# Queries of two pairs of heads in one product of 384 columns, and a new written order for layer 1's input and attention

## The chip, the cores and the metric

One core of one Trainium2 chip runs the whole program in one launch. The metric is the device time of one execution in microseconds (us), the median of the runs. The core has four engines that matter here: TensorE (PE in the profile; the load of its weights is PEld), VectorE (DVE), ScalarE (ACT) and GpSimd (POOL); SyncE (SP) issues most transfers.

## The reference

Two layers of a transformer block on 512 tokens of width 1024, conditioned by a vector, beside 256 tokens of context. Cut to the parts of layer 1 that the change touches:

```python
# layer 0: Fourier and Hyena mixer and feed-forward network, for x (512 tokens) and ctx (256)
# layer 1: attention for x over x and ctx, then the feed-forward network for x
a_x = hx @ w_in                                   # 256 for queries, 128 + 32 for keys and values
q = (_rms_norm(a_x[..., :256], q_a_norm) @ w_uq).reshape(B, L, 16, 96)
q = _rms_norm(q, q_norm)                          # over the 96 of each head
q = concat([q[..., :64], _rope_2d(q[..., 64:], rope)])
kv = (_rms_norm(a_kv[..., :128], kv_a_norm) @ w_ukv).reshape(B, L, 16, 64 + 64)
k = _rms_norm(concat([kv[..., :64], k_pe for all heads]), k_norm)   # with rope where it is x
s = einsum('bqhd,bkhd->bhqk', q, k) * 96 ** -0.5  # 16 heads, 512 queries, 768 keys
o = einsum('bhqk,bkhv->bqhv', softmax(s), v)
x = x + g1 * (o @ w_o)
```

All is fp32.

## The kernel before

**Products.** A fp32 number is split in two fp32r parts, hi (on ACT, L296) and lo (on DVE, L301), and a product is three products of the parts (`mm3`, L321, L322, L323). So each weight is loaded to `wr`, converted to `wh` and subtracted to `wl` before TensorE can use it.

**Stages.** Layer 0 and its feed-forward network come first (to about 820 us), then layer 1's input (low-rank products of queries and keys/values, norms, tables of rotation), then attention (905 to 1114), then the feed-forward network. The order of every engine's instructions is the order in which the program calls its steps: tables of step names are written out as strings, and the tile scheduler is told to keep that order (`manual_schedule`). `IN2_ORDER` holds the steps from the end of layer 0's down-projection to the start of attention, with the down-projection's own products (DP), the low-rank products (QA, KV, PE) and the loads among them; `ORDER` holds attention. There are four such blocks in the program before; in the block of `ORDER` SP is not among the engines that keep the written order, so the scheduler places its loads.

**Attention.** The 16 heads go as 8 pairs, numbered 0 to 7 behind the step's name (`QT.3`). For a pair:

- LW, WA, WD load and split the weights w_uq, for two pairs at a time (L309, L296, L301).
- QT multiplies the query's low-rank tiles `qah`, `qal` (two halves of 256 rows) by the weights, for four tiles of 128 tokens, 192 columns each: 4 x 2 x 3 = 24 products into the PSUM tile `k2` (one buffer, 1024 columns, also used by UK). In the trace they are `k<-wh,qah` and its like.
- SQ squares the result (ACT), RD sums it (DVE, L1926), TB (L1918) and TX (L1922) multiply it with the tables `tabm` and `tabx` into the tile `t2`. TB, TX and SQ free `k2`.
- UK makes the pair's keys into `k2`; KSQ, KS, KH, KL square, sum and split them. NA, NB, RT make the norms' factors, U scales the queries, TR transposes them (TensorE), QC and QL split them.
- SC makes the scores of 128 keys by 512 queries (6 steps for each of two heads), EV scales and moves them to SBUF (ACT), MA, MB, MD, AR find the maxima, SU subtracts, EX is the exponential (ACT).
- VP and VE make the values. PW (L2062) multiplies values and exponentials, ON (L2073) sums the exponentials: both are column-tiled, four products of 32 rows of output side by side (128*32 in the profile), six steps each for a pair. A step shows as 8 records.
- ZC copies the sums, ZA brings them through DRAM into 128 x 8, RC is the reciprocal, ZB and ZD bring it back spread over the rows (tile R), DV multiplies (tile O), OH and OL split the result.
- LX, XA, XD load and split the output weights w_o; WO multiplies.

RP.1 (L1867) and RP.0 (L1864) are thin products that place the rotated part of the keys, `kp`, and its sums.

```python
def QT(c, p):
    c.q = K2()
    wh, wl = wq[p // 2]
    for t_ in range(4):
        for k in range(2):
            s, w = slice(128 * t_, 128 * t_ + 128), slice(384 * (p % 2) + 192 * k, ...)
            self.mm3(c.q[:, 256 * t_ : 256 * t_ + 192], qah[k][:, s], qal[k][:, s], wh[:, w], wl[:, w], k == 0, k == 1)
```

Of the kernel before, what the change touches and what calls it, by code (L numbers as in the profile page):

```python
# [21 lines left out]
P = 128  # L22
D = 1024
KD = 8
# [27 lines left out]
SU11.2 ZD.1 SC11.3 EV10.3 KS.4 EV11.3 MA0.3 KH0.4 SC12.3 KH1.4 KL0.4 SC13.3 EX10.2 SC14.3 NA.4 MB0.3 QT.5 EX11.2 DV.1 MD0.3 NB.4 EV12.3 WD.6 ON0.2
AR0.3 ON1.2 EV13.3 RT.4 ON2.2 LX2.7 EV14.3 ON3.2 MA1.3 ON4.2 U1.4 ON5.2 PW0.2 U0.4 SQ.5 SU00.3 PW1.2 ZC.2 TR1.4 OH.1 ZA.2 TR0.4 XA1.7 RD.5 SC15.3 TB.5
QC0.4 PW2.2 QC1.4 QL0.4 PW3.2 EV15.3 TX.5 EX00.3 PW4.2 MB1.3 PW5.2 OL.1 SC00.4 MD1.3 SC01.4 EV00.4 RC.2 SC02.4 AR1.3 SU01.3 EV01.4 ZB.2 SC03.4 EV02.4
UK.5 EV03.4 XD1.7 ZD.2 EX01.3 SC04.4 MA0.4 SC10.4 LX0.7 EV04.4 SC05.4 SU10.3 KSQ.5 SC11.4 EV10.4 KS.5 EV05.4 SU11.3 EX10.3 SC12.4 SC13.4 DV.2 EV11.4
NA.5 PW0.3 EX11.3 MB0.4 ON0.3 ON1.3 NB.5 ON2.3 MD0.4 EV12.4 PW1.3 RT.5 AR0.4 EV13.4 SC14.4 U0.5 KH0.5 MA1.4 TR0.5 U1.5 ON3.3 PW2.3 KL0.5 QC0.5 ON4.3
SU00.4 EV14.4 PW3.3 KH1.5 ON5.3 PW4.3 OH.2 QL0.5 ZC.3 PW5.3 KL1.5 EX00.4 ZA.3 SC15.4 OL.2 SC00.5 SU01.4 EV15.4 TR1.5 EV00.5 SC01.5 QC1.5 MB1.4 QT.6
EV01.5 EX01.4 QL1.5 RC.3 MD1.4 ZB.3 SC02.5 TB.6 SQ.6 AR1.4 SC03.5 EV02.5 RD.6 ZD.3 SC10.5 EV03.5 SC04.5 TX.6 EV10.5 MA0.5 UK.6 EV04.5 SU10.4 SC11.5
KSQ.6 SC05.5 EV11.5 KS.6 SU11.4 EV05.5 EX10.4 SC12.5 NA.6 SC13.5 DV.3 EX11.4 SC14.5 MB0.5 SC15.5 EV12.5 ON0.4 PW0.4 MD0.5 NB.6 EV13.5 RT.6 AR0.5 PW1.4
KH0.6 MA1.5 ON1.4 U1.6 PW2.4 U0.6 ON2.4 KL0.6 KH1.6 ON3.4 PW3.4 EV14.5 SU00.5 PW4.4 EV15.5 OH.3 ON4.4 MB1.5 ON5.4 EX00.5 TR0.6 TR1.6 SU01.5 QT.7 QC0.6  # L60
QC1.6 ZC.4 QL0.6 EX01.5 ZA.4 MD1.5 PW5.4 TB.7 AR1.5 SQ.7 SC00.6 OL.3 XA0.7 SC01.6 TX.7 EV00.6 SC02.6 RD.7 EV01.6 SC03.6 RC.4 EV02.6 SU10.5 ZB.4 SC04.6
EV03.6 SC10.6 EV04.6 SC05.6 SU11.5 ZD.4 EX10.5 UK.7 EV10.6 SC11.6 MA0.6 KSQ.7 SC12.6 XD0.7 EV05.6 KS.7 EX11.5 MB0.6 ON0.5 ON1.5 EV11.6 NA.7 ON2.5 DV.4
EV12.6 SC13.6 MD0.6 NB.7 KH0.7 ON3.5 RT.7 AR0.6 ON4.5 EV13.6 U0.7 SC14.6 U1.7 KL0.7 TR0.7 ON5.5 MA1.6 EV14.6 PW0.5 QC0.7 SU00.6 PW1.5 KH1.7 PW2.5 ZC.5
# [179 lines left out]
class Builder:  # L243
# [2478 lines left out]
```

## Time and profile before

| | us |
|---|---|
| median of 3 runs (1493.09 to 1493.64) | 1493.27 |
| the profiled execution | 1492.97 |
| its span | 1491.2 |
| TensorE busy | 1468.9 (99%) |
| DVE busy | 1257.8 (84%) |
| ACT busy | 727.4 (49%) |
| POOL busy | 230.0 (15%) |
| mean granted clock of TensorE | 0.994 |

The span runs from the first to the last instruction that the profiler saw; 1.8 us of the execution lie outside it. A row of TensorE's timeline gives start, length and shape; matmuls overlap in the records, so the time that one takes is read from the start of one to the start of the next. Where a row ends with [..], the engine was idle that long ahead of it, and what it names ended the idle time.

### The profile page before, as it was taken

The page shows a single profiled execution, that of the slowest core. Times are in us where ns is not written, and L with a number is a line of the kernel's source. Part 1 is how long each engine was busy: PE and PEld are TensorE (multiplying, and loading weights), DVE is VectorE, ACT ScalarE, POOL GpSimd, SP SyncE. Part 2 cuts the span into 40 slices and gives each one's busy share as a digit, 9 for nine tenths or more (in the row PEclk, how much of TensorE's full clock was granted, in tenths as well). Part 3 has the DMA queues.
Part 4 walks back from the last instruction along what each step waited for, and adds up shares of the span by engine and source line. Part 5 has one row for each costly group of instructions (what it writes and reads, how often), then busy time and mean ns, then how long its engine had stood idle before and what let it go on. Part 6 is the DMA issues. An engine that isn't in the chain of part 4 may idle for free.

```text
span 1491.2 us, 24094 instructions
## 1 busy us (share of the span) xinstructions
PE 1468.9 (99%) x9216; PEld 1279.2 (86%) x9216; DVE 1257.8 (84%) x2118; ACT 727.4 (49%) x1117; POOL 230.0 (15%) x396
## 2 busy tenths in 40 slices
PE   7999999999999999999999999999999999999998
PEld 4778889798999999999999888665659999989997
DVE  6899999999988988778878777899957997878885
ACT  3452234355443344334344347988936554444442
POOL 0101043011112121121220000111111221212100
PEclk8999999999999999999999999999999999999999
DMA  8425543764477787778887440010035566555543
GB/s 334 147 92 179 201 151 106 236 210 121 106 195 181 195 206 183 176 211 215 212 212 248 138 139 26 23 32 20 16 110 167 137 168 154 148 158 149 142 108 119
DMA packets 89903, 226.36 MB, mean 152 GB/s; under 512 B 12955, under 2 KB 20605, under 8 KB 88765
## 3 DMA queue, kind: packets, MB, share of 16 engines
q1 hardware_dynamic: 64573, 161.28, 32.3%
q0 software_dynamic: 25216, 63.55, 19.7%
q8 instruction: 72, 1.18, 0.3%
q14 instruction: 42, 0.34, 0.1%
HBM read 203.15 MB, written 21.64 MB: 151 GB/s over the span
## 4 chain that ended last, share of the span: by engine, by line
PE 87%; DVE 7%; DMA 2%; ACT 2%; issue 1%; SPq 0%; POOL 0%; DVEq 0%; ACTq 0%; POOLq 0%
PE mm L321 21%; PE mm L323 21%; PE mm L322 21%; PE ms L323 3%; PE ms L321 3%; PE ms L322 3%; PE pv L2062 3%; PE s L2010 1%; PE pv L2073 1%; DVE wl L301 1%; PE s L321 1%; DMA sb<-wmodT 1%; PE s L322 1%; DVE junk L420 1%; PE s L323 1%
## 5 line engine op out<-in xcount | busy, mean ns | idle before, releaser
L296 ACT ACTIVATE wh<-wr 128x1024 fp32r<-128x1024 f32 (+4 forms) x179 | 153.2, 861 | 195.2 <-PE mm L322 89.8
L321 PE MATMUL mm<-hh,wh 128*128 128x512 f32 (+3 forms) x704 | 230.8, 328 | 0.7 <-ACT pt L1750 0.7
L322 PE MATMUL mm<-hl,wh 128*128 128x512 f32 (+3 forms) x704 | 228.6, 325 | 0.0
L323 PE MATMUL mm<-hh,wl 128*128 128x512 f32 (+3 forms) x704 | 227.9, 324 | 0.1
L301 DVE TENSOR_TENSOR wl<-wr,wh 128x1024 fp32r<-128x1024 f32 (+4 forms) x179 | 174.8, 981 | 47.6 <-ACT wh L296 47.2
L321 PEld LDWEIGHTS mm<-hh,wh 128*128 128x128 f32 x704 | 133.2, 189 | 12.2 <-issue 2.7
L322 PEld LDWEIGHTS mm<-hl,wh 128*128 128x128 f32 x704 | 133.2, 189 | 8.5 <-issue 0.4
L323 PEld LDWEIGHTS mm<-hh,wl 128*128 128x128 f32 x704 | 132.9, 189 | 8.7 <-DVE wl L301 0.8
L420 DVE SCALAR_TENSOR_TENSOR junk<-wr,sb 128x1024 bf16<-128x1024 f32 x96 | 116.9, 1218 | 4.2 <-DMA wr<-wmodT 4.1
L323 PE MATMUL ms<-hh,wl 128*128 128x386 f32 (+2 forms) x240 | 76.2, 317 | 1.5 <-DVE wl L301 1.5
L321 PE MATMUL ms<-hh,wh 128*128 128x386 f32 (+2 forms) x240 | 76.1, 317 | 0.3 <-DVE fg L1460 0.3
L322 PE MATMUL ms<-hl,wh 128*128 128x386 f32 (+2 forms) x240 | 76.0, 317 | 0.0
L321 PE MATMUL mm<-x,wh 128*128 128x512 f32 (+1 forms) x224 | 76.0, 339 | 0.0
L322 PE MATMUL mm<-x,wh 128*128 128x512 f32 (+1 forms) x224 | 76.0, 339 | 0.0
L323 PE MATMUL mm<-x,wl 128*128 128x512 f32 (+1 forms) x224 | 75.6, 338 | 0.0
L322 PE MATMUL mm<-al,wh 128*128 128x512 f32 x176 | 69.6, 396 | 0.0
L323 PE MATMUL mm<-ah,wl 128*128 128x512 f32 x176 | 69.6, 396 | 0.0
L321 PE MATMUL mm<-ah,wh 128*128 128x512 f32 x176 | 69.6, 395 | 0.0
L2018 ACT ACTIVATE S<-s,rks 128x512 f32<-128x512 f32 x96 | 61.8, 694 | 5.8 <-PE s L2010 2.4
L2031 POOL PARTITION_ALL_REDUCE mx<-mx x16 | 34.0, 2130 | 194.6 <-DVE mx L2028 166.2
L296 ACT ACTIVATE wh<-sum 128x1024 fp32r<-128x1024 f32 x40 | 42.4, 1059 | 41.8 <-PE mm L322 19.9
L2284 POOL DMA_DIRECT2D sum<-w_up x40 | 23.6, 615 | 221.6 <-DVE wl L301 84.5
(548 smaller groups left out, 4366.1 us busy)
## 6 DMA issues: line engine op xcount, KB each, us to landing
wr<-wmodT SPq DMA_DIRECT2D x48, 512.0 KB, 3.8
wr<-w_up SPq DMA_DIRECT2D x48, 512.0 KB, 3.5
sum<-w_up POOLq DMA_DIRECT2D x80, 256.0 KB, 4.3
sb<-wmodT SPq DMA_DIRECT2D x32, 512.0 KB, 4.4
xs<-delta POOLq DMA_DIRECT2D x32, 386.0 KB, 7.3
wr<-w_dn SPq DMA_DIRECT2D x48, 256.0 KB, 4.6
sa<-w_up POOLq DMA_DIRECT2D x40, 256.0 KB, 5.0
sb<-w_up POOLq DMA_DIRECT2D x40, 256.0 KB, 5.1
```

The lines of the kernel that those rows point to most:

```text
L296: self.nc.scalar.activation(dst, src, AF.Copy)
L301: (eng or self.nc.vector).tensor_tensor(dst, src, hi.bitcast(F32), op=ALU.subtract)
L321: mmul(out, wh, xh, start=start, stop=False)
L322: mmul(out, wh, xl, start=False, stop=False)
L323: mmul(out, wl, xh, start=False, stop=stop)
L420: nc.vector.scalar_tensor_tensor(junk, raw, 1.0, self.sb[j], op0=ALU.mult, op1=ALU.mult, accum_out=acc)
L2010: nc.tensor.matmul(ps, Kf[:, tok[j] : tok[j] + 128], q[0], start=True, stop=True)
L2018: nc.scalar.activation(c.S[a][:, j, :], c.ps[a, j], AF.Copy, scale=c.r[:, g : g + 1])
L2031: nc.gpsimd.partition_all_reduce(c.m[a][:, 1, :], c.m[a][:, 0, :], P, bass.bass_isa.ReduceOp.max)
L2062: nc.tensor.matmul(c.P[r : r + 32, :], V[:, j, 128 * p + r : 128 * p + r + 32], c.S[a][:, j, :], start=c.np == 0, stop=c.np == 5, tile_pos ...
L2073: nc.tensor.matmul(c.Z[o : o + 32, 0:256], ones, c.S[a][:, j, 256 * h : 256 * h + 256], start=c.nz == 0, stop=c.nz == 5, tile_position=(0, o))
L2284: nc.gpsimd.dma_start(t_[:, 512:1024], g[:, 0:512])
```

## The change

**Queries of a group.** Two pairs make a group. QT of an even pair now makes the queries of both pairs for the first two tiles of tokens, QT of the odd pair for the last two: 2 x 2 x 3 = 12 products of 384 columns instead of 24 of 192. The host lays w_uq out so that the 384 columns lie together. SQ, RD and TX work on as many elements as before; TB is two instructions of 128 x 384 instead of one of 128 x 768. Both halves of a group have to be done before either of its pairs can go on to NA and U.

**One tile for z, R and O.** ZC, ZD and DV use one tile of 512 columns, DV in place, instead of three.

**The order.** `IN2_ORDER` and `ORDER` are new throughout. QT.1 and its SQ, TB, TX, RD stand in `IN2_ORDER`, ahead of UK.0. The steps of PW and ON are spread among the products of scores. One `manual_schedule` encloses both layers, with SP in all of it; loads stand where the tables name them, and the last split of w_o (XA3, XD3) stands at the table's end.

Numbers of instructions: TensorE has 96 fewer, DVE 4 rows more; ACT, POOL and SP have as many as before. In layer 0 ahead of its last down-projection and in the feed-forward network behind attention each engine has the same rows in the same order.

```diff
         def QT(c, p):
-            c.q = K2()
+            g, h = groups[p // 2], p % 2
+            g.q = K2()
             wh, wl = wq[p // 2]
-            for t_ in range(4):
+            for j in range(2):
                 for k in range(2):
-                    s, w = slice(128 * t_, 128 * t_ + 128), slice(384 * (p % 2) + 192 * k, 384 * (p % 2) + 192 * k + 192)
-                    self.mm3(c.q[:, 256 * t_ : 256 * t_ + 192], qah[k][:, s], qal[k][:, s], wh[:, w], wl[:, w], k == 0, k == 1)
-            c.q = c.q.rearrange("p (t f) -> p t f", t=4)
+                    s, w = slice(128 * (2 * h + j), 128 * (2 * h + j) + 128), slice(384 * k, 384 * k + 384)
+                    self.mm3(g.q[:, 512 * j : 512 * j + 384], qah[k][:, s], qal[k][:, s], wh[:, w], wl[:, w], k == 0, k == 1)
+            g.q = g.q.rearrange("p (t f) -> p t f", t=2)
...
         def TB(c, p):
-            c.t = self.t(pq, [P, 4, 320], F32, "t2")
-            v.tensor_tensor(c.t.rearrange("p t (a f) -> p t a f", a=2)[:, :, :, 0:96], c.q[:, :, 0:192].rearrange("p t (a f) -> p t a f", a=2),
-                            tabm.rearrange("p t (a f) -> p t a f", a=2), op=ALU.mult)
+            g, h = groups[p // 2], p % 2
+            if h == 0:
+                g.t = self.t(pq, [P, 4, 2, 256], F32, "t2")
+                for e in range(2):
+                    pairs[p + e].t = g.t[:, :, e, :]
+            for a in range(2):
+                o, w = 160 * a, slice(96 * a, 96 * a + 96)
+                v.tensor_tensor(g.t[:, 2 * h : 2 * h + 2, :, o : o + 96], g.q[:, :, 0:384].rearrange("p t (e f) -> p t e f", e=2)[:, :, :, w],
+                                tabm[:, 2 * h : 2 * h + 2, w].rearrange("p t (o f) -> p t o f", o=1).to_broadcast([P, 2, 2, 96]), op=ALU.mult)
...
         def ZC(c, p):
-            c.z = self.t(pq, [P, 256], F32, "z")
+            c.R = self.t(pq, [P, T], F32, "R")
+            c.z = c.R[:, 0:256]
             nc.scalar.copy(c.z, c.Z[:, 0:256])
...
         def DV(c, p):
-            c.O = self.t(pq, [P, T], F32, "O")
+            c.O = c.R
             v.tensor_tensor(c.O, c.P, c.R, op=ALU.mult)
...
-        with self.tc.manual_schedule(engines={ENG.PE, ENG.DVE, ENG.Activation, ENG.SP, ENG.Pool}):
-            for s in IN2_ORDER.split():
+        for s in IN2_ORDER.split():
...
-    r["w_uq"] = uq.transpose(0, 4, 1, 3, 2, 5).reshape(4, P, 768)
+    r["w_uq"] = uq.transpose(0, 4, 3, 1, 2, 5).reshape(4, P, 768)
```

The order of TensorE at the start of attention, before: QT.0 (12 of its 24 products left out), the thin products, two steps of values (`pv`), then UK.0 (`k_1802`).

```order
L321 MATMUL k_1795_9260<-wh_9096,qah_1710_8864 128x192
L322 MATMUL k_1795_9260<-wl_9097,qah_1710_8864 128x192
L323 MATMUL k_1795_9260<-wh_9096,qal_1712_8866 128x192
...
L322 MATMUL k_1795_9260<-wl_9097,qah_1711_8865 128x192
L323 MATMUL k_1795_9260<-wh_9096,qal_1713_8867 128x192
L1867 MATMUL s_9262<-kp_9228,msk_8876 128x512
L1867 MATMUL s_9263<-kp_9228,msk_8876 128x260
L1864 MATMUL s_9261<-ones_3_71,sqpe_9226 128x1 x6
L321 MATMUL pv_9259<-wh_9085,kvh_8862 128x512
...
L321 MATMUL pv_9360<-wh_9085,kvh_8862 128x512
...
L321 MATMUL k_1802_9319<-kvh_8862,wh_9201 128x512
...
L321 MATMUL k_1802_9319<-kvh_8862,wh_9201 128x260
```

After: QT.0 in 12 products of 384, RP.1, QT.1, RP.0, UK.0, then the values.

```order
L322 MATMUL k_1795_9258<-wh_9154,qah_1707_8869 128x384
L323 MATMUL k_1795_9258<-wl_9155,qah_1707_8869 128x384
L324 MATMUL k_1795_9258<-wh_9154,qal_1709_8871 128x384
...
L324 MATMUL k_1795_9258<-wh_9154,qal_1710_8872 128x384
L1863 MATMUL s_9260<-kp_9242,msk_8881 128x512
L1863 MATMUL s_9261<-kp_9242,msk_8881 128x260
L322 MATMUL k_1802_9290<-wh_9154,qah_1707_8869 128x384
...
L324 MATMUL k_1802_9290<-wh_9154,qal_1710_8872 128x384
L1860 MATMUL s_9259<-ones_3_71,sqpe_9231 128x1 x6
L322 MATMUL k_1804_9324<-kvh_8867,wh_9105 128x512
...
L322 MATMUL k_1804_9324<-kvh_8867,wh_9105 128x260
...
L322 MATMUL pv_9257<-wh_9191,kvh_8867 128x512
```

QT.1 (`k_1802_9290`) moved in between the two kinds of thin products, and UK.0 ahead of the values; the tile k2 is used three times in a row.

DVE at the same place, before: `kp` ahead of the second half of the rotation tables, then TB.0 (L1918), RD.0, TX.0 (L1922).

```order
L1807 SCALAR_TENSOR_TENSOR pt_9220<-mm_8969,pcol_67,pt_9218 128x256
L1859 SCALAR_TENSOR_TENSOR kp_9228<-mm_8937,pcol_67,ropeK_8880 64x772
L301 TENSOR_TENSOR kvl_8863<-pt_9220,kvh_8862 128x256
L1807 SCALAR_TENSOR_TENSOR pt_9239<-mm_8969,pcol_67,pt_9237 128x512
L1779 TENSOR_TENSOR tabx_8874<-tabx_8874,gg_8881 128x256
L1779 TENSOR_TENSOR tabm_8873<-tabm_8873,gg_8881 128x768
L301 TENSOR_TENSOR kvl_8863<-pt_9239,kvh_8862 128x512
L1918 TENSOR_TENSOR t_1800_9308<-k_1795_9260,tabm_8873 128x8x96
L1926 TENSOR_REDUCE rd_s_9310<-sq_9291 128x8
L1922 TENSOR_TENSOR t_1800_9308<-k_1795_9260,tabx_8874 128x4x64
```

After:

```order
L1803 SCALAR_TENSOR_TENSOR pt_9225<-mm_8983,pcol_67,pt_9203 128x256
L1775 TENSOR_TENSOR tabm_8878<-tabm_8878,gg_8886 128x768
L1775 TENSOR_TENSOR tabx_8879<-tabx_8879,gg_8886 128x256
L1803 SCALAR_TENSOR_TENSOR pt_9239<-mm_8983,pcol_67,pt_9210 128x512
L1855 SCALAR_TENSOR_TENSOR kp_9242<-mm_8922,pcol_67,ropeK_8885 64x772
L1922 TENSOR_TENSOR t_1799_9279<-k_1795_9258,tabm_8878 128x4x96 x2
L1927 TENSOR_TENSOR t_1799_9279<-k_1795_9258,tabx_8879 128x4x64
L302 TENSOR_TENSOR kvl_8868<-pt_9225,kvh_8867 128x256
...
L1936 TENSOR_REDUCE rd_s_9288<-sq_9286 128x8
L1922 TENSOR_TENSOR t_1799_9279<-k_1802_9290,tabm_8878 128x4x96 x2
```

`kp` moved behind both tables, directly ahead of TB.0, and the splits of the keys' and values' tile (`kvl`) behind it; TB.1 follows.

The outputs of pair 0 on TensorE, before: a sum of squares (L1955), five steps of PW, two of ON, then PW and ON to their end, then transposes (L1990). Left-out rows are further steps of the same kind.

```order
L321 MATMUL s_9717<-q_1878_9624,K_1716_8870 128x512
...
L1955 MATMUL s_9722<-msk_8876,sq_9698 128x2 x6
L2062 MATMUL pv_9732<-S_9483,V_9254 32x512 x2
L2062 MATMUL pv_9732<-S_9534,V_9254 32x512 x2
...
L2073 MATMUL pv_9774<-S_9483,msk_8876 32x256 x2
L2073 MATMUL pv_9774<-S_9534,msk_8876 32x256 x2
...
L1990 MATMUL s_9815<-cst_69,t_1882_9638 128x128 x4
```

After: three steps of ON, a triple of scores, then one more step of ON, two of PW and two of ON (the first rows of PW are shown), and scores again.

```order
L1965 MATMUL s_9684<-msk_8881,sq_9674 128x2 x6
L2083 MATMUL pv_9696<-S_9484,msk_8881 32x256 x2
L2083 MATMUL pv_9696<-S_9508,msk_8881 32x256 x2
...
L322 MATMUL s_9711<-q_1876_9583,K_1713_8875 128x512
L323 MATMUL s_9711<-ql_1886_9615,K_1713_8875 128x512
L324 MATMUL s_9711<-q_1876_9583,K_1714_8876 128x512
...
L2072 MATMUL pv_9719<-S_9484,V_9252 32x512 x2
L2072 MATMUL pv_9719<-S_9508,V_9252 32x512 x2
...
L322 MATMUL s_9766<-q_1876_9583,K_1713_8875 128x512
L323 MATMUL s_9766<-ql_1886_9615,K_1713_8875 128x512
```

What was one run of column-tiled products is cut by scores in several places. Over the whole of attention there were 20 such runs, and there are 37.

SP in layer 1's input, before: the loads of w_dn (`wr`) that the stretch around 821 us waits for stand among the loads of the residual (`xr`).

```order
L1604 DMA sb_1627_8367<-wmodT 128x1024
L1242 DMA xr_1632_8399<-xs_599_2872 128x772
L1242 DMA xr_1634_8401<-xs_597_2870 128x772
L1242 DMA xr_1635_8402<-xs_596_2869 128x772
L309 DMA wr_8422<-w_dn 128x768
L1242 DMA xr_1631_8398<-xs_600_2873 128x772
L1242 DMA xr_1638_8405<-xs_593_2866 128x772
L309 DMA wr_8448<-w_dn 128x768
L1242 DMA xr_1637_8404<-xs_594_2867 128x772
L1604 DMA sb_1650_8516<-wmodT 128x1024
```

After:

```order
L1600 DMA sb_1627_8367<-wmodT 128x1024
L1238 DMA xr_1638_8405<-xs_593_2866 128x772
L1238 DMA xr_1631_8398<-xs_600_2873 128x772
L1238 DMA xr_1634_8401<-xs_597_2870 128x772
L1238 DMA xr_1636_8403<-xs_595_2868 128x772
L1600 DMA sb_1646_8500<-wmodT 128x1024
L1238 DMA xr_1632_8399<-xs_599_2872 128x772
L1238 DMA xr_1635_8402<-xs_596_2869 128x772
L310 DMA wr_8504<-w_dn 128x768
L310 DMA wr_8506<-w_dn 128x768
L1600 DMA sb_1655_8557<-wmodT 128x1024
```

The first `wr` moved behind six `xr` and one `sb`, and a second follows directly.

More of the change, by code (lines that the diff above doesn't have):

```diff
@@ L70 @@
+XD3.7
 """
@@ L2481, in ffn_blocks @@
         more.update(CO=CO, RF=RF, HF=HF, LF=LF, UF=UF)
-        with self.tc.manual_schedule(engines={ENG.PE, ENG.DVE, ENG.Activation, ENG.SP, ENG.Pool}):
-            for s in IN1_ORDER.split():
-                name, *args = s.split(".")
-                (more[name] if name in more else one[name])(*[int(n) for n in args])
-            for s in UP_ORDER.split():
-                step(s)
+        for s in IN1_ORDER.split():
+            name, *args = s.split(".")
+            (more[name] if name in more else one[name])(*[int(n) for n in args])
+        for s in UP_ORDER.split():
+            step(s)
         for n in ("blk", "ftm1", "act1"):
@@ L2494, in build @@
         self.setup()
-        x = self.layer1(*self.layer0())
+        ENG = mybir.EngineType
+        with self.tc.manual_schedule(engines={ENG.PE, ENG.DVE, ENG.Activation, ENG.Pool, ENG.SP}):
+            x = self.layer1(*self.layer0())
         for d in range(KD):
```

134 lines of the change are left out of this document (68 added, 66 removed).

## The prediction

> **What bounds the kernel now.** I read the page's engine line first, then the busy time by stretch for the part of the program that the change rewrites (the end of layer 0's second half to the end of attention), then the chain of waits on TensorE, then the instructions of TensorE one by one at the places that the waits name.
>
> ```profile
> PE 1468.9 (99%) x9216; PEld 1279.2 (86%) x9216; DVE 1257.8 (84%) x2118; ACT 727.4 (49%) x1117; POOL 230.0 (15%) x396
> ```
> TensorE is busy 99% of the span: what counts is the number and length of its products, and what little it waits.
>
> The next view has, per stretch, its length and then the busy time of PE, PEld, DVE, ACT and POOL, the granted clock, the DMA share and GB/s.
>
> ```profile
> 800.00:840.00 40.00, 38.62 (x173) 31.79 (x173) 27.41 (x44) 13.62 (x18) 0.00 (x0) 1.00 0.58 205
> 880.00:905.00 25.00, 24.31 (x160) 20.76 (x160) 18.35 (x37) 10.85 (x22) 0.00 (x0) 0.93 0.15 49
> 905.00:1078.00 173.00, 172.30 (x1243) 115.17 (x1242) 153.95 (x191) 151.43 (x238) 27.80 (x14) 1.00 0.07 23
> 1078.00:1114.00 36.00, 35.84 (x266) 18.46 (x265) 18.21 (x20) 14.63 (x18) 6.18 (x2) 1.00 0.25 84
> ```
> The attention loop (905 to 1078) leaves TensorE idle 0.7 us, with DVE at 89% and ACT at 88%: there the order of the work matters, but little is left to win. Three idle or slow places lie ahead of the loop; TensorE's waits (total, times, longest) name them:
>
> ```profile
> PE mm L321 <- ACT wh L296: 1.1, 1, 1.1
> PE mm L321 <- ACT pt L1750: 0.7, 1, 0.7
> PE k L321 <- DVE t L1922: 0.5, 1, 0.5
> PE mm L323 <- DVE wl L301: 0.3, 1, 0.3
> PE s L1955 <- ACT sq L1936: 0.2, 1, 0.2
> PE pv L2073 <- ACT S L2040: 0.2, 1, 0.2
> ```
> So the whole region holds 3.0 us of named waits. Beyond these only shorter products, or a faster clock, can win time there.
>
> **Part 1, the query product (QT).** It goes from 24 products of 192 columns per pair to 12 of 384. Rows of TensorE's timeline (start, length, line, operation); starts are what counts, since lengths overlap:
>
> ```profile
> 929.14 0.40 PE L323 MATMUL pv<-wh,kvl 128*128 128x512 f32 x1
> 929.37 0.25 PE L321 MATMUL k<-wh,qah 128*128 128x192 f32 x1
> ...
> 932.03 0.42 PE L321 MATMUL s<-q,K 128*128 128x512 f32 x1
> ```
> A 512-column product takes 0.23 us from start to start; the 24 narrow ones take 932.03 - 929.37 = 2.66, so 0.111 each, well over 192/512 of 0.23 (0.086). The trace of before has no product of 384 columns; the nearest are layer 1's 386-column ones:
>
> ```profile
> 781.97 0.34 PE L321 MATMUL mm<-T2h,wh 128*128 128x386 f32 x1
> ...
> 787.82 0.34 PE L321 MATMUL mm<-T4h,wgh 128*128 128x386 f32 x1
> ```
> 33 steps in 5.85 us: 0.177 each, 0.176 at 384 columns. Twelve take 2.12; a pair saves 0.54, eight pairs 4.4 us, all of it on TensorE's path. Bounds: nothing saved if a 384 cost what two 192 do (0.222); 4.7 if it cost 384/512 of the 0.23 (12 x 0.1725 = 2.07, 0.59 a pair). The 386-column row is nearest, so 4.4.
>
> [...]
>
> **Part 2, PW and ON, cut finer.** These are the column-tiled products (128*32). Between full-array products a run of them costs more than its records:
>
> ```profile
> 1087.38 0.40 PE L323 MATMUL s<-Oh,wl 128*128 128x512 f32 x1
> 1087.71 1.92 PE L2062 MATMUL pv<-S,V 128*32 128x512 f32 x16
> ...
> 1089.91 0.40 PE L322 MATMUL k<-Ol,wh 128*128 128x512 f32 x1
> ...
> 1090.84 0.40 PE L323 MATMUL k<-Oh,wl 128*128 128x512 f32 x1
> 1091.17 1.06 PE L2062 MATMUL pv<-S,V 128*32 128x512 f32 x8
> ...
> 1092.50 0.40 PE L322 MATMUL k<-Ol,wh 128*128 128x512 f32 x1
> ```
> From the product ahead to the second one behind: 2.53 us with 16 records, 1.66 with 8. Eight records are then 0.87 (0.109 each), and 1.66 - 0.87 - 2 x 0.23 = 0.33 is the price of one run, whatever its length. Counted in the order of the program, runs of PW and ON go from 20 to 37: 17 x 0.33 = +5.6 us. Bounds: 0.15 a run if only one of its two borders costs (+2.6), 0.34 (+5.8). No row excludes the lower, but both runs shown paid in full, so 5.6.
>
> **Part 3, the waits ahead of the loop.** SP now issues w_dn's load behind six xr loads and one of sb, where it stood behind three xr. The place today:
>
> ```profile
> 821.01 0.40 PE L323 MATMUL mm<-x,kl 128*128 128x512 f32 x1
> 822.52 0.50 PE L321 MATMUL mm<-a,wh 128*128 128x512 f32 x1 [1.11 <-ACT wh L296]
> ```
> and on ACT:
> ```profile
> 821.62 0.84 ACT L296 ACTIVATE wh<-wr 128x768 fp32r<-128x768 f32 x1 [7.83 <-DMA wr<-w_dn]
> ```
> 1.51 less 0.23 is 1.3 lost, and 0.3 for wl (the waits): 1.6. In the new order some 30 more products (30 x 0.23, 7 us) stand ahead of the one that needs these weights, against four more loads on SP ahead of the transfer. I take the 1.6 as gone; the other end is that it only moves (0).
>
> ```profile
> 886.39 0.28 PE L323 MATMUL mm<-hh,wl 128*128 128x260 f32 x1
> 887.36 0.39 PE L321 MATMUL mm<-hh,wh 128*128 128x260 f32 x1 [0.69 <-ACT pt L1750]
> ```
> 0.97 less 0.12 for a product: 0.85, which goes since other columns of the low-rank products now stand there. The three waits of the loop (0.5, 0.2, 0.2) belong to an order that is gone: 0.9. Together -3.4 us; ends -1.7 and -3.4.
>
> **Part 4, the clock.** Windows of 1 us, columns as above; the granted clock is third from the end:
>
> ```profile
> 901.00:902.00 1.00, 1.00 (x5) 0.79 (x5) 0.97 (x3) 0.00 (x0) 0.00 (x0) 0.62 0.00 0
> 902.00:903.00 1.00, 1.00 (x4) 0.81 (x3) 0.92 (x4) 0.84 (x2) 0.00 (x0) 0.50 0.00 0
> 903.00:904.00 1.00, 1.00 (x3) 0.79 (x3) 0.97 (x3) 0.38 (x1) 0.00 (x0) 0.50 0.00 0
> 904.00:905.00 1.00, 1.00 (x5) 0.79 (x4) 1.00 (x2) 0.00 (x0) 0.00 (x0) 0.68 0.00 0
> ```
> 0.38 + 0.50 + 0.50 + 0.32 = 1.7 us lost. Just ahead stand the thinnest products of the region:
> ```profile
> 898.14 1.56 PE L1867 MATMUL s<-kp,msk 64*128 64x512 f32 x4
> 899.63 1.49 PE L1864 MATMUL s<-ones,sqpe 32*128 32x1 f32 x12
> ```
> 2.9 us of them in one piece. The change puts QT.1, 2.1 us of full products, between the two. I take the loss as gone, -1.7; the other end is 0, since 1.5 us of thin products still stand on each side and a wait may widen them. [...]
>
> **Part 5, what the change adds in waits.** DVE's product of q with its table is one instruction of 768 elements and becomes two of 384. On DVE (a group of one shape: busy, mean ns; then instructions in time):
>
> ```profile
> L1918 DVE TENSOR_TENSOR t<-k,tabm 128x768 f32<-128x768 f32 x7 | 6.7, 955 | 3.7 <-PE k L323 2.5 <-ACT sq L1913 1.1
> ```
> ```profile
> 895.53 1.01 DVE L1859 SCALAR_TENSOR_TENSOR kp<-mm,pcol,ropeK 64x772 f32<-64x772 f32 x1 [0.65 <-ACT sqpe L1855]
> ...
> 896.80 0.73 DVE L1807 SCALAR_TENSOR_TENSOR pt<-mm,pcol,pt 128x512 f32<-128x512 f32 x1
> 897.47 0.41 DVE L1779 TENSOR_TENSOR tabx<-tabx,gg 128x256 f32<-128x256 f32 x1
> 897.80 0.94 DVE L1779 TENSOR_TENSOR tabm<-tabm,gg 128x768 f32<-128x768 f32 x1
> ```
> 256 elements take 0.41 and 768 take 0.94, so an instruction has about 0.15 fixed: two of 384 are 1.10, +0.15 for each of eight steps, 1.2 us on DVE, which had 19 us free in the loop: nothing on TensorE's path unless the next user of the PSUM tile comes sooner. That user is the new wait. The tile k2 has one buffer; QT and UK share it, and now a second QT follows the first before any UK. Between them TensorE has 15 products of 0.23 at QT.2 to QT.3 (3.5 us) and 12 at QT.5 to UK.4 (2.8); DVE needs 1.10 + 0.41 = 1.5 to read the tile out. 2.8 - 1.5 = 1.3 us of lateness on DVE is covered.
>
> At the start it is not. kp moves behind tabm, tabx and pt: 2.08 later on DVE. Before it was done at 896.54 and used at 898.14, 1.6 in hand; QT.0 is 0.54 shorter. 1.6 - 2.08 - 0.54 = -1.0; but DVE was idle 0.65 ahead of kp, which these steps can now fill: -0.4. I take 0.4 us of wait ahead of the L1867 products, between 0 and 1.0. UK.0 then waits for TX.1 on k2: 1.5 of reading against 1.5 of L1864's thin products: 0.2. For the remainder of the loop, whose order is wholly new, I take 1.5; the ends are 0 and 5 (0.9 at each of six QT that follow another user of k2 closely).
>
> At the end of attention the last pair's outputs take:
> ```profile
> 1097.51 0.37 ACT L2079 COPY z<-pv 128x256 f32<-128x256 f32 x1 [1.63 <-PE pv L2073]
> ...
> 1109.69 0.69 DVE L301 TENSOR_TENSOR Ol<-O,Oh 128x512 fp32r<-128x512 f32 x1 [0.70 <-ACT Oh L296]
> ```
> 12.9 us from copying the sums to the last part of O. TensorE now has, behind the last ON, six PW steps (5.2), four extra runs (1.3) and 14 triples of 512 columns for the output (9.8): 16.3 before it needs that O. z, R and O share a tile, so pair 7's copy waits for pair 6's last step, some 16 us of TensorE's work earlier. Nothing waits; if the cover were gone, 1 us of lateness costs 1 us.
>
> Instructions elsewhere are the same and in the same order; joining the blocks adds none, so I cost that at nothing, since no row shows a cost at the blocks' borders.
>
> **Sum.** -4.4 + 5.6 - 3.4 - 1.7 + (0.4 + 0.2 + 1.5) = -1.8. The profiled execution took 1492.97, 0.3 below the median of 1493.27; so 1491.2 in its terms and 1491.5 against the median.
>
> **The rivals.** *The stalls go and the finer cut is cheap.* Runs cost 0.15 (+2.6), nothing new but the waits for kp and at UK.0 (0.6): -4.4 + 2.6 - 3.4 - 1.7 + 0.6 = -6.3, 1487.0. For it: many of the new runs are short ON runs, not shown alone in before; against it: both measured runs paid 0.33. With runs at 0.25 (+4.3) it is 1488.7.
> *k2 decides (slower).* Place: each second QT of a group and the UK behind it. If DVE is over 1.3 us late there, TensorE waits; DVE at 89% with steps of 1 us makes one step of lateness likely, two decide. 0.9 at six places instead of 1.5 in all, and the half clock back (+1.7): -1.8 + 3.9 + 1.7 = +3.8, 1497.1. For it: one such wait (0.5, on t of L1922) stands in before already; against it: only one of eight.
> *384 columns save nothing.* A 384 costs what two 192 do: 4.4 is missing, +2.6, 1495.9. [...] The 386-column row speaks against it.
>
> **How the numbers follow.** A measurement of this kernel can tell about 0.2%, 3.0 us, from no change. No change to be told (1490.3 to 1496.3), with 1491.5 likeliest: 0.43. Stalls gone and cheap runs, 1487.0 to 1490.2: 0.33. k2 decides: 0.19. Nothing saved by width: 0.05, inside no change. So faster 0.33, same 0.48, slower 0.19. The range goes from 1486.7 (the low ends: -4.7 + 2.6 - 3.4 - 1.7 + 0.6 = -6.6) to 1497.0 (new waits of 5.9 and the half clock kept: -4.4 + 5.6 - 3.4 + 5.9 = +3.7). The likeliest case's own range is 1490.3 to 1494.5.
>
> **What would show it.** QT: 12 products from start to start, 2.1 us. The wait on wh ahead of 830 gone; a new one on kp ahead of the thin products. The clock 1.00 around UK.0. Runs of 128*32 products with 0.33 over their records, the ON runs above all: if they show 0.15, the faster case holds. Waits of k on t (DVE) add up to over 4 us if k2 decides. I am wrong altogether if a wait of several us opens in the loop where DVE or ACT fall behind the new order.

## The result, and the profile after

The changed kernel is slower: 1501.4 us against 1493.5 (medians of six runs each), a ratio of 1.0053 with a 95% interval of 1.0037 to 1.0068, so 5.5 to 10.2 us. Its profiled execution took 1498.8 (span 1497.0) against 1493.0 (span 1491.2).

```profile
PE 1472.0 (98%) x9120; PEld 1272.8 (85%) x9120; DVE 1257.1 (84%) x2126; ACT 727.0 (49%) x1117; POOL 232.7 (16%) x396
```
DVE has eight instructions more (2126 against 2118), since each TB is two now.

The same stretches as before (length; PE, PEld, DVE, ACT, POOL busy; granted clock; DMA share; GB/s):

```profile
800.00:840.00 40.00, 40.00 (x183) 33.20 (x182) 29.12 (x47) 13.72 (x19) 0.10 (x4) 1.00 0.66 233
880.00:905.00 25.00, 22.15 (x146) 18.81 (x145) 17.86 (x37) 13.03 (x26) 0.00 (x0) 0.99 0.16 49
905.00:1078.00 173.00, 171.48 (x1137) 106.87 (x1137) 148.97 (x196) 147.05 (x233) 30.94 (x14) 0.99 0.07 22
1078.00:1114.00 36.00, 35.60 (x261) 17.36 (x261) 19.76 (x19) 15.77 (x20) 5.75 (x2) 1.00 0.20 64
```
The idle time around 821 is gone (40.00 of 40); 2.85 us idle stand at the start of attention instead, where it was 0.7, and 1.5 in the loop. TensorE's waits from 815 to 1150 name them:

```profile
PE k L322 <- ACT sq L1912: 2.2, 2, 1.2
PE pv L2083 <- DVE R L2110: 1.0, 1, 1.0
PE mm L322 <- ACT pt L1746: 0.7, 1, 0.7
PE ms L458 <- DVE nt L452: 0.4, 1, 0.4
PE pv L2083 <- ACT S L2050: 0.4, 1, 0.4
PE k L322 <- DVE K L302: 0.3, 1, 0.3
PE s L1965 <- ACT sq L1946: 0.2, 1, 0.2
```
The largest is one that the prediction did not have: `k`, the queries' and keys' tile k2, waits for ACT's squares. On TensorE's timeline:

```profile
894.80 0.34 PE L322 MATMUL k<-wh,qah 128*128 128x384 f32 x1
...
896.74 0.34 PE L324 MATMUL k<-wh,qal 128*128 128x384 f32 x1
897.01 1.56 PE L1863 MATMUL s<-kp,msk 64*128 64x512 f32 x4
899.78 0.44 PE L322 MATMUL k<-wh,qah 128*128 128x384 f32 x1 [1.21 <-ACT sq L1912]
...
902.07 1.49 PE L1860 MATMUL s<-ones,sqpe 32*128 32x1 f32 x12
904.50 0.79 PE L322 MATMUL k<-kvh,wh 128*128 128x512 f32 x1 [0.95 <-ACT sq L1912]
```
QT.0's twelve products take 0.176 each (1.94 in eleven steps), as foretold. Then TensorE waits 1.2 us ahead of QT.1 and 0.95 ahead of UK.0. What reads k2 in between stands on DVE

```profile
897.17 1.02 DVE L1922 TENSOR_TENSOR t<-k,tabm 128x384 f32<-128x384 f32 x2 [0.32 <-PE k L324]
898.11 0.42 DVE L1927 TENSOR_TENSOR t<-k,tabx 128x256 f32<-128x256 f32 x1
898.44 1.02 DVE L302 TENSOR_TENSOR kvl<-pt,kvh 128x256 fp32r<-128x256 f32 x2
...
902.17 1.02 DVE L1922 TENSOR_TENSOR t<-k,tabm 128x384 f32<-128x384 f32 x2 [1.46 <-PE k L324]
```
and on ACT

```profile
898.92 0.81 ACT L1912 ACTIVATE sq<-k 128x768 f32<-128x768 f32 x1 [2.40 <-PE s L1863]
...
903.64 0.81 ACT L1912 ACTIVATE sq<-k 128x768 f32<-128x768 f32 x1 [2.56 <-PE s L1860]
```
ACT is idle for 2.4 us and begins only when DVE has read the tile (until 898.53): the two engines read it one after the other, QT.0's from 897.17 to 899.73 and QT.1's from 902.17 to 904.45. The releasers that the two ACT rows name are the thin products; these end within 0.04 us of DVE's last reading (898.57 and 903.56), so at these two places the rows alone do not say which of the two ACT waited for. The rows of before do, for the loop: there ACT's squares wait for DVE's product, and DVE's for ACT's squares.

```profile
L1913 ACT ACTIVATE sq<-k 128x768 f32<-128x768 f32 x7 | 5.7, 808 | 6.2 <-DVE t L1918 5.0 <-PE k L323 1.2
L1922 DVE TENSOR_TENSOR t<-k,tabx 128x256 f32<-128x256 f32 x7 | 2.9, 418 | 0.5 <-ACT sq L1913 0.5
```
Some 0.3 of QT.0's 2.6 us is no reading. SQ.0 begins 0.39 after DVE's last reading, where SQ.1 begins 0.11 after it, and between them DVE does the first split of `kvl` (0.41 in before, so until 898.85); e4_start names that split as what SQ.0 waited for (2.41 <-DVE kvl).

The granted clock (third column from the end) falls to half behind the second wait, as it did before behind the thin products, some 3.3 us earlier (0.62 from 901 to 902 there):

```profile
904.00:905.00 1.00, 0.49 (x1) 0.50 (x2) 0.97 (x2) 1.00 (x3) 0.00 (x0) 0.76 0.00 0
905.00:906.00 1.00, 1.00 (x4) 0.71 (x4) 0.97 (x2) 0.45 (x1) 0.00 (x0) 0.50 0.00 0
906.00:907.00 1.00, 1.00 (x5) 0.93 (x4) 0.00 (x1) 0.16 (x1) 0.00 (x0) 0.50 0.00 0
907.00:908.00 1.00, 1.00 (x4) 0.79 (x3) 0.00 (x0) 1.00 (x2) 0.00 (x0) 0.53 0.00 0
```
0.24 + 0.50 + 0.50 + 0.47 = 1.7 us lost, the same as before.

Whole times of one kernel spread over 3 to 12 us, and much of that arises ahead of anything edited here: the last 386-column product of layer 0 starts between 808.6 and 814.2 us in the profiled executions, although the program is the same up to it. So the experiments are read first by a stretch that every one has and that holds the edits: from QT.0's first product to the last product of the output weights. Before, its ends are

```profile
895.31 0.34 PE L321 MATMUL k<-wh,qah 128*128 128x192 f32 x1
...
1143.52 0.28 PE L323 MATMUL mm<-Oh,wl 128*128 128x256 f32 x1
```
and after 894.80 and 1148.94:

```profile
1148.94 0.28 PE L324 MATMUL mm<-Oh,wl 128*128 128x256 f32 x1
```
248.2 us before and 254.1 after: +5.9. From layer 0's last 386-column product up to QT.0 it is 86.7 and 85.7: -1.1. This part differs from trace to trace by itself: in the experiments below it takes 87.2 to 87.6 with the order of before (with one piece of half clock taken out of e3_split's 88.9) and 85.0 to 86.9 with the new one; the means lie 1.5 apart.

### The profile page after: what moved, and what is told of

Same layout as the page of the kernel before. It is cut to its first block, busy times and chain, and to the rows that moved or that the text cites. A ratio compares the mean times of both kernels' runs of the same rounds, so it can differ in the third digit from the quotient of the medians.

```text
span 1497.0 us, 23928 instructions
## 1 busy us (share of the span) xinstructions
PE 1472.0 (98%) x9120; PEld 1272.8 (85%) x9120; DVE 1257.1 (84%) x2126; ACT 727.0 (49%) x1117; POOL 232.7 (16%) x396
## 4 chain that ended last, share of the span: by engine, by line
PE 78%; DVE 12%; ACT 3%; DMA 3%; issue 2%; POOL 1%; SPq 0%; DVEq 0%; ACTq 0%; POOLq 0%
PE mm L322 20%; PE mm L324 20%; PE mm L323 20%; PE ms L324 3%; PE ms L322 3%; PE ms L323 3%; DVE wl L302 2%; DVE junk L421 1%; DVE S L2046 1%; DMA sb<-wmodT 1%; POOL mx L2041 1%; PE pv L2072 1%; DMA wr<-wmodT 1%; DVE mx L2035 1%; PE k L322 1%
## 5 line engine op out<-in xcount | busy, mean ns | idle before, releaser
L322 PEld LDWEIGHTS mm<-hh,wh 128*128 128x128 f32 x704 | 133.5, 190 | 12.2 <-issue 2.7
L2046 DVE TENSOR_TENSOR S<-S,mx 128x1536 f32<-128x1536 f32 x32 | 55.2, 1746 | 7.6 <-POOL mx L2041 7.6
```

What stands on the lines that cost most here:

```text
L322: mmul(out, wh, xh, start=start, stop=False)
L2046: v.tensor_tensor(s, s, mb.to_broadcast([P, 3, T]), op=ALU.subtract)
```

## Experiments

Each kernel's stretch from QT.0 to the last output product, what the half clock lost in it (the sum over windows of 1 us of one less the granted clock), and the ratio of the whole time to the kernel before with the 95% interval (none for two kernels that were profiled only). A stretch is one trace's, so differences of the half clock have to be taken out before two stretches are compared.

| kernel | stretch, us | of it half clock | ratio |
|---|---|---|---|
| before | 248.2 | 1.7 | 1 |
| after | 254.1 | 1.7 | 1.0053 (1.0037 to 1.0068) |
| e1_w192, after with 192 columns | 257.9 | 1.7 | 1.0058 (1.0039 to 1.0077) |
| e2_runs20, after with 20 runs | 260.4 | 5.1 | 1.0077 (1.0059 to 1.0095) |
| e3_split, before with 37 runs | 253.5 | 1.7 | 1.0032 (1.0015 to 1.0049) |
| e4_start, after with values ahead of UK.0 | 253.9 | 1.7 | 1.0025 (1.0012 to 1.0038) |
| e5_oneblock, before as one block | 248.7 | 1.7 | 0.9994 (0.9980 to 1.0007) |
| e6_q384, before with 384 columns | 271.1 | 10.2 | 1.0149 (1.0129 to 1.0169) |
| e7_thin, before with values between thin products | 246.5 | 0 | 0.9992 (0.9977 to 1.0007) |
| e8_runs28, after with 28 runs | 256.2 | 5.1 | 1.0025 (1.0008 to 1.0042) |
| e9_input, e7_thin with the new input order | 246.8 | 0 | 0.9992 (0.9976 to 1.0007) |
| e10_sq, after with SQ off k2 | 250.2 | 0 | - |
| e11_dv, after with DV.2 ahead | 253.1 | 1.7 | - |
| e12_close, three edits on after | 247.5 | 0 | 0.9986 (0.9974 to 0.9998) |

**The width alone (e1_w192).** On the changed kernel:

```diff
-self.mm3(g.q[:, 512 * j : 512 * j + 384], ..., wh[:, w], wl[:, w], k == 0, k == 1)
+for e in range(2):  # before k; w is 192 columns of the 384
+    self.mm3(g.q[:, 512 * j + 192 * e : 512 * j + 192 * e + 192], ..., wh[:, w], wl[:, w], k == 0, k == 1)
```


> The changed kernel with QT's products cut back to 192 columns (24 a half group, same PSUM tile, same order of everything else). Theory A (TensorE is the bound and every product counts, the parts add up): QT goes from 0.176 to 0.111 x 2 per 384 columns, 8 x 0.55 = +4.4 us over the changed kernel, so about 1.0082 of the kernel before; the waits behind QT stay as they are. Theory B (the new order is bound by what ACT and DVE hand over, TensorE waits in any case): the longer QT is taken out of the waits, under +1 us, about 1.0055.

The 192 narrow products take 22.2 us from start to start where the 96 wide ones took 17.7 (+4.5), and the stretch is 3.8 longer. Theory A: the width is worth some 4 us on the path, and 0.7 of it went into waits that became shorter (ON's on DV.2, 1.0 to 0.5; the sum of squares of the keys, 0.2 to none). Whole times do not bear theory A out: its 1.0082 lies outside the interval of the ratio, which is 1.0058, hardly over the changed kernel's 1.0053 and on theory B's 1.0055. So the 4 us are the trace's.

**The borders of PW and ON (e3_split, e2_runs20, e8_runs28).** On the kernel before, single steps moved in `ORDER`:

```diff
-PW4.0 ... PW5.0 ... ON5.0 ... TR0.2 TR1.2
+... ON5.0 ... TR0.2 PW4.0 TR1.2 PW5.0
...
```


> The kernel before with 17 single steps of PW moved behind the next products of scores, transposes or queries, so that its 20 runs become 37; QT and all else as before the change. Theory A: +17 borders at 0.29 (next to transposes) to 0.33, +5.3 us, 1.0035 of the kernel before. Theory B (borders are hidden in an order bound by ACT and DVE): within 1 us, 1.000.

+5.3 us in the stretch, 0.31 for each of 17 new runs, with no new wait in the loop and the half clock the same in both: the price read off two runs of before holds for 17.

The other way round, on the changed kernel:

```diff
-ON0.0 ON1.0 ON2.0 ... SC12.1 ON3.0
+... SC12.1 ON0.0 ON1.0 ON2.0 ON3.0
...
```


> The changed kernel with steps of PW and ON moved later on TensorE until they stand in 20 runs, as many as before the change, instead of 37; nothing else is moved. Theory A (each run of column-tiled products costs 0.33 at its borders): 17 x 0.33 = -5.6 us against the changed kernel, 1.0015 of the kernel before; in the trace the 128*32 runs show 0.33 over their records each. Theory B (the new order is bound by ACT and DVE): within 1 us of the changed kernel, 1.005, as the borders come back as waits; or slower, if the later ends of PW and ON hold up what follows.

6.3 us longer instead of shorter. The 17 borders are gone, but TensorE's waits (905 to 1125) are now

```profile
PE s L1999 <- ACT S L2027: 3.3, 1, 3.3
PE s L1999 <- DVE t L1992: 2.2, 1, 2.2
PE s L321 <- DVE ql L301: 1.7, 1, 1.7
PE pv L2082 <- ACT S L2049: 1.1, 1, 1.1
PE s L2019 <- ACT S L2027: 1.1, 1, 1.1
```
In the new order PW and ON cover the time in which ACT and DVE prepare what the next products need; moved behind those products, they cover it no longer (named waits of 12.2 us in the stretch against 4.1). The wait of 3.3 us ends with ACT's L2027, a move of scores that frees a PSUM tile (EV); in ACT's order such moves stand there behind two exponentials and a scaling. The half clock costs more besides, 5.1 us in the stretch against 1.7. Of it 1.7 lie between 906 and 911, and behind the wait of 3.3 us 24 records of PW take 3.54 us (1000.49 to 1004.03), 0.147 each, where 8 more of them took 0.87, 0.109 each, in before. As a direct test of the borders the run failed, but an estimate from its parts agrees with their price: TensorE's named waits in the stretch went from 4.1 to 12.2 us and the half clock from 1.7 to 5.1, which leaves 6.3 - 8.1 - 3.4 = -5.2 for 17 runs, 0.31 each. The next run makes only the moves behind which nothing had waited:

> The changed kernel with nine pieces of PW and ON moved later on TensorE past one product each (a triple of scores, a transpose or a triple of outputs), so that 37 runs become 28; the moves of the 20-run kernel behind which TensorE waited for ACT's scores are left out. Theory A (0.33 a run where nothing waits for the moved piece): 9 x 0.33 = -3.0 us from QT.0 to the last output product (254.1 to 251.1), 1.0033. Theory B (later ends of PW and ON come back as waits, as in the 20-run kernel): 0 or slower, 1.0053 and above.

The stretch is 256.2, but here the half clock lasted from 907 to 917.5, three times as long, though the two programs are the same up to there:

```profile
907.00:908.00 1.00, 1.00 (x7) 0.81 (x6) 0.92 (x2) 0.58 (x2) 0.00 (x0) 0.86 0.00 0
...
917.00:918.00 1.00, 1.00 (x5) 0.82 (x5) 0.00 (x0) 0.61 (x1) 0.00 (x0) 0.52 0.00 0
```
That is 5.1 us lost against 1.7. Without the difference it is 252.8, 1.3 less than after, where nine borders would give 3.0; 0.7 came back as a wait for `ql` and 0.5 in two waits that were there before. Between the theories; with the 1.2 of waits taken out, the nine borders gave 2.5, 0.28 each.

**The start of attention (e4_start, e10_sq).**

```diff
-... RD.0 QT.1 RP.0 ... RL.1   (then UK.0, and VP40.0 VP50.0 in ORDER)
+... RD.0 VP40.0 QT.1 RP.0 ... RL.1 VP50.0   (then UK.0)
```


> The changed kernel with two steps of values (VP) moved ahead: one between the thin products RP.1 and QT.1, one between RP.0 and UK.0, where TensorE waited for the PSUM tile k2. Theory A: the waits of 1.2 and 0.95 us there are covered, -1.5 us, and the clock no longer falls to half behind them, as no thin stretch is over 1.6 us, -1.5 us more: -3 in all, 1.0033 of the kernel before. Theory C (the half clock does not come from these thin products and idle spots but falls at this place in any case): the clock still goes to 0.5 around 905 and it is -1.5 us, 1.0043.

The waits for k2 fell from 2.2 to 0.3, but the stretch by only 0.2. The next product of the chain waits instead, KS for the squares of the keys, and the clock falls to half from 909.7 on, behind that wait:

```profile
906.98 0.28 PE L323 MATMUL k<-kvh,wl 128*128 128x260 f32 x1
908.17 1.50 PE L1964 MATMUL s<-msk,sq 128*128 128x2 f32 x12 [0.90 <-ACT sq L1945]
```
Theory C, and more: here the cover put in front of a chain of read-outs moved the wait along the chain, from k2 to KS (0.90). The ratio, 1.0025, is better than the changed kernel's, from another chip and other runs; the stretch does not bear it out. Then the suspected cause itself was taken away:

```diff
-nc.scalar.activation(g.qs.rearrange("p (t f) -> p t f", t=2), g.q[:, :, 0:384], AF.Square)
+nc.scalar.activation(g.qs.rearrange("p (t f) -> p t f", t=4), tabm, AF.Square)
```


> The changed kernel with SQ squaring the table tabm instead of the queries in k2, of the same size, so that only DVE reads that PSUM tile (the norms of the queries are then not those of the reference). Theory E (ACT's SQ waits until DVE has read k2 and k2 is free only after both, 2.7 us instead of the 1.5 that the prediction counted): the waits of 1.2 us ahead of QT.1 and 0.95 ahead of UK.0 go or fall below 0.3 each. Theory F (DVE alone holds k2 too long): they stay.

```profile
901.64 1.56 PE L1863 MATMUL s<-kp,msk 64*128 64x512 f32 x4
903.30 0.41 PE L322 MATMUL k<-wh,qah 128*128 128x384 f32 x1
...
905.55 1.49 PE L1860 MATMUL s<-ones,sqpe 32*128 32x1 f32 x12
907.16 0.47 PE L322 MATMUL k<-kvh,wh 128*128 128x512 f32 x1
```
QT.1 and UK.0 follow the thin products with no wait, the clock stays 1.00, and the stretch is 3.9 shorter: 2.2 for the waits and 1.7 for the clock. Theory E: without ACT's reading the tile is free in time. That ACT reads late because DVE reads first is shown by the rows in the section on the result (in before, 5.0 us of ACT's idle time ahead of SQ ended with DVE's product), not by this run, which takes the reading away altogether.

**DV.2 behind a step that waits (e11_dv).**

```diff
-SU00.4 DV.2 EX10.3
+DV.2 SU00.4 EX10.3
```


> The changed kernel with DV.2 moved ahead of SU00.4 on DVE, nothing else. Theory A (the wait of 1.0 us ahead of ON0.3 is DV.2 standing behind a step that waits 1.7 us for POOL's maximum): that wait goes, -1 us from QT.0 to the last output product. Theory B (DV.2's factor from DRAM is not there sooner): DV.2 waits for the transfer, the wait stays.

On DVE after, DV.2 (`R<-pv,R`) stands behind a subtraction that waits for POOL's maximum, until 1021.92, and with it the PSUM tile that ON0.3 needs:

```profile
1019.56 1.76 DVE L2046 TENSOR_TENSOR S<-S,mx 128x1536 f32<-128x1536 f32 x1 [1.68 <-POOL mx L2041]
1021.24 0.68 DVE L2110 TENSOR_TENSOR R<-pv,R 128x512 f32<-128x512 f32 x1
```
In the experiment it runs in the idle time:

```profile
1018.08 0.68 DVE L2110 TENSOR_TENSOR R<-pv,R 128x512 f32<-128x512 f32 x1
1019.84 3.43 DVE L2046 TENSOR_TENSOR S<-S,mx 128x1536 f32<-128x1536 f32 x2 [1.08 <-POOL mx L2041]
```
The wait is gone and the stretch 1.0 shorter. Theory A.

**One block (e5_oneblock).** The kernel before with one `manual_schedule` in `build` in place of four, tables as they were.

> The kernel before with nothing changed but that one block of written order encloses both layers (SP in it); the tables are those of before. On TensorE this puts UK.0 ahead of two steps of values, which the scheduler had moved in front of it at the border of two blocks, and fixes SP's loads in attention. Theory A (the prediction's: joining the blocks costs nothing): within 1 us of the kernel before, 1.000. Theory D (the border had given UK.0 its cover): TensorE waits for k2 ahead of UK.0, from the end of the thin products to the end of the tile's reading, about 0.6 us, and the norms behind it come no sooner: +0.5 to +1.5 us from QT.0 to the last output product, 1.0006.

UK.0 now stands ahead of the two steps of values and waits 0.66 us for k2 (on t, DVE); the stretch is 0.5 longer. Theory D in the trace, 0.5 us; in whole times no difference that can be told (0.9994). In the prediction this part stood at nothing.

**The queries alone (e6_q384).** On the kernel before, QT to NA of the changed kernel, and per group:

```diff
-QT.2 ... TX.2 ... RD.2 ... UK.2 KSQ.2 ... KS.2 ... QT.3 ... TB.3 ... SQ.3 ... TX.3 ... RD.3
+QT.2 ... TX.2 ... RD.2 SC02.1 QT.3 ... SC03.1 TB.3 SQ.3 TX.3 RD.3 ... UK.2 KSQ.2 ... KS.2
...
```


> The queries' part alone: the kernel before with QT, SQ, TB, TX, RD and NA of the changed kernel (384 columns, groups of two pairs); the second QT of a group and its readers stand a few products of scores behind the first, UK, KSQ and KS behind that; QT.1 stands behind UK.0. PW, ON and the blocks as before (20 runs). z, R and O share a tile as in the change, but for pair 7, whose z has a tile of its own; the splits of O stand a little earlier. Theory A (parts add up): -4.3 us at QT, less new waits for the tile k2 of 1 to 2: 1490 to 1492, 0.998. Theory B (both halves are needed before a pair can go on, so grouping costs at the start and at each group what the width brings): 0 to +3 us, 1.000 to 1.002.

22.9 us longer, far outside both; 8.5 of it is half clock (10.2 us lost against 1.7). The largest waits in attention:

```profile
PE s L2004 <- DVE t L1997: 4.2, 2, 3.6
PE s L321 <- ACT q L296: 2.4, 2, 1.4
PE s L321 <- ACT S L2032: 1.2, 1, 1.2
PE s L1969 <- ACT sq L1950: 1.2, 3, 0.8
PE s L322 <- DVE ql L301: 1.1, 2, 0.9
PE k L321 <- DVE K L301: 1.1, 1, 1.1
```
Transposes (L2004) wait for the scaled queries, scores for transposed ones, UK for k2. The second QT and its read-out stand in the chain of the first pair. It was one placing by simple rules; it shows that the grouping needs a new order, not that no order could carry it.

**The clock (e7_thin, e9_input).** On the kernel before, VP40 and VP50 between RP.1 and RP.0:

```diff
-RP.1 RT.0.0 RT.0.1 RT.1.0 RP.0
+RP.1 RT.0.0 RT.0.1 RT.1.0 VP40.0 VP50.0 RP.0
```


> The kernel before with two steps of values (VP40, VP50) written between the thin products RP.1 and RP.0, so that they no longer stand in one piece of 2.9 us. Theory A (a stretch of 2.9 us of thin products sets the clock to half): the clock stays 1.00 around 905, -1.5 us, 0.999 of before. Theory C (any thin or idle stretch near here does it): UK.0 now stands right behind RP.0 with KS soon after, the half clock falls a few us later and nothing is won, 1.000.

```profile
895.00:905.00 10.00, 10.00 (x66) 8.14 (x64) 9.10 (x18) 6.07 (x11) 0.00 (x0) 1.00 0.13 42
905.00:915.00 10.00, 9.92 (x68) 8.68 (x67) 7.42 (x15) 7.91 (x16) 0.00 (x0) 1.00 0.00 0
```
The clock stays at 1.00 and the stretch is 1.7 shorter: theory A. With layer 1's input in the changed kernel's order besides:

```diff
-IN2_ORDER of before
+IN2_ORDER of after, without QT.1 SQ.1 TB.1 TX.1 RD.1, with VP40.0 VP50.0 ahead of RP.0
```


> The kernel before with two things: the changed kernel's order of layer 1's input (without QT.1, which stays in attention) and two steps of values between the thin products RP.1 and RP.0. Attention's order, QT of 192 columns and 20 runs as before. Theory A (the parts add up): 1.1 us less up to QT.0, as between the two kernels, since the wait for w_dn's weights goes, and 1.7 from QT.0 to the last output product, since the clock stays up: -2.8, 0.998. Theory B (what is won ahead of attention comes back as waits on ACT or DVE at its start): -1 or less, 0.9995.

From layer 0's last 386-column product to QT.0 85.6 (before 86.7), the stretch behind 246.8: -2.5 together, theory A in the trace. Both ratios, 0.9992 with intervals over 1, leave it open whether the whole is faster.

**The account closed (e12_close).** e10_sq, e11_dv and e8_runs28 in one kernel.

> The changed kernel with three edits together: SQ squares the table tabm instead of the queries in k2 (the norms are then not the reference's), DV.2 ahead of SU00.4, and the nine merges of PW and ON (28 runs). Theory A (the parts add up): from QT.0 to the last output product 254.1 less 3.9 (k2 and the clock), 1.0 (DV.2) and 1.2 to 3.0 (nine runs; the 28-run kernel's own, without its longer half clock, was 1.2): 246 to 248, at or under the 248.2 of before. Theory B (waits return elsewhere as others are removed): over 249.5.

247.5: theory A. Hardly any wait came back elsewhere (0.5 of k on K, 0.4 for ql), and 0.9986 (0.9974 to 0.9998) is a little under the kernel before. But before loses 1.7 us to the half clock in this stretch and this kernel none: against e7_thin, which is before with the clock kept up (246.5), it is still 1.0 longer. As in e10_sq its norms are of a table, so it is no version to use; it shows that what the change lost to waits is what these edits remove.

## Why the prediction was wrong, step by step

It said 1491.5, between 1486.7 and 1497.0; the median is 1501.4, and "slower" had 0.19.

| term | predicted | measured | from |
|---|---|---|---|
| QT of 384 columns | -4.4 | -4.3; -3.8 on the path | starts of QT's products, 22.0 to 17.7; e1_w192 |
| 17 more runs of PW and ON | +5.6 | +5.3 | e3_split |
| waits ahead of QT.0 | -2.5 | -1.1 (-1.5 by the means of all traces) | the traces |
| half clock | -1.7 | 0 | the two traces |
| waits from QT.0 on, old and new | -0.9 + 2.1 | the remainder: about +4.9 | 5.9 + 4.3 - 5.3 |

The two terms on which most of the working rested were right. The step that failed is "DVE needs 1.10 + 0.41 = 1.5 to read the tile out". ACT's SQ reads k2 too, and the two engines do not read it at the same time: 1.44 and 0.81 make 2.3 us from first to last at QT.1 (902.17 to 904.45), and 2.6 at QT.0, where DVE splits `kvl` in between. In none of the 16 read-outs of queries in the two traces do they overlap (the closest are 0.03 us apart, as SQ at 933.22 in before behind TB, which ends at 933.19); at the start of attention in after, ACT's SQ begins 0.39 and 0.11 us behind DVE's last reading. The rows were there in before: among the releasers of TB stands "ACT sq 1.1" in the row that the prediction quotes, and I took SQ as running beside it.

From the reading in turn follow three of the misses. UK.0's wait was put at 0.2 and was 0.95. The wait ahead of QT.1, 1.2, was not in the sum at all, which had a wait for kp in its place (0.4) that did not come. And the clock, to be kept up by QT.1's full products between the thin ones, met 1.5 us of thin products with 0.95 of waiting behind them: e10_sq without the waits keeps it at 1.00. That the split alone would keep the clock up was my estimate, which no row of before shows; the changed kernel lost the same 1.7 us, and e7_thin, with the thin products apart and no wait behind them, lost none. So 3.9 us hang on one PSUM tile. The sum had 0.6 for waits at this place, where 2.2 came, and -1.7 for the clock, where 0 came: 3.3 of the 7.6 us by which it missed the profiled execution (+5.8 against -1.8). The rival "k2 decides" named the tile and the sign, with the wrong ground (a late DVE) and the wrong place (the later groups, where six places together show 0.3).

The other misses are small. The wait for pt (0.69) stood unchanged, now at 885.57, though I had it go with the order, and 0.44 came ahead of L458. The wait for w_dn's weights went, as said. The waits of the loop, put at 1.5, are 1.9, of which 1.0 is DV.2's (e11_dv). TensorE's named waits in the stretch grew from 0.9 to 4.1, by 2.2 for k2 and 1.0 for DV.2; so about 1.7 of the table's last 4.9 stand in no named wait, and no experiment took them apart. Joining the blocks, put at nothing, took two steps of values from in front of UK.0 (0.5 by e5_oneblock, a part of the 0.95 here). The 5.9 of new waits at the range's upper end is no sum of the ends given for its parts (1.0 + 0.2 + 5 = 6.2, which would make 1497.3); the measured time lies above either.

The whole time moved by 7.9 between medians, the part from the last 386-column product to the last output product by 4.9 in the traces. The intervals allow 5.5; by the two traces the remainder lies where the programs do not differ, and I leave it open.

## What to carry to other kernels

Count every engine that reads a PSUM tile before calling the tile's next use covered: here DVE (1.44 us) and ACT (0.81) read k2 one after the other, and its three uses in a row brought waits of 1.2 and 0.95 us. A wider product is worth its shorter stream only if the order that it asks for costs less: here the width was worth 4 us, and with both halves of the queries at the head of the chain the waits for their tile cost 2.2 and the half clock behind them 1.7. Where products of another tiling stood among full ones, each of their runs had a price (0.31 us in e3_split), and merging them paid only where nothing waited then for what they covered (e2_runs20: 5.2 won by estimate, 8.1 more of waits). Before two traces are compared, look at the granted clock in both: here it made up to 8.5 us of a difference (e6_q384).

## What was new of the hardware

Between layer 0's last 386-column product and the last output product, what the 14 traces lost to the half clock comes in pieces of 1.7 us, each some 3.4 us at a clock of 0.50 (1.7 / 0.50): none in e7_thin, e9_input, e10_sq and e12_close, one in before, after, e1_w192, e4_start, e5_oneblock and e11_dv, two in e3_split, three in e2_runs20 and e8_runs28, six in e6_q384. In before, after and e4_start it came behind 2.4 to 2.9 us of thin products and waiting together; behind 1.5 us of thin products alone, with full ones on both sides (e7_thin, e10_sq), the clock stayed at 1.00, and so it did behind the 1.6 us of RP.1 with 1.2 us of waiting right behind it, after. TensorE was busy by its rows for all of the 2.9 us in before, and for 1.5 of the 2.4 in after and e4_start. In these traces the length alone does not tell where a piece comes: 2.4 us had one behind it, 2.8 had none.

The program alone does not fix where a piece falls. e3_split has one around 896, ahead of everything edited, where before runs the same instructions at 1.00 (0.50 from 897 to 899 in e3_split); e8_runs28 has three in a row, 5.1 us, where after has one. So a single trace does not tell 1.7 us from chance; the readings above rest on all four kernels with the thin products apart and no wait behind them keeping the clock up at the start of attention, and all ten others losing it there. The spread of whole times goes with it too: of 29 runs of the kernel before on one chip, the 7 with a mean granted clock of 0.996 or 0.997 have a median of 1494.5 us, the 8 with 0.992 or 0.993 one of 1499.9.
